# Two changes of order at the end of the second layer: the last third of the token sums goes to POOL's queue behind the last scan, and the weight splits wait for the root of the last pair's normalisation

## The chip, the cores and the metric

The kernel runs as one program on one core of a Trainium2 chip. The metric is the device time of one execution in microseconds (us). Each number below that belongs to an execution is that of the kernel before: three timed runs, and one more that the hardware profiler recorded. The engines are named as the profile names them: PE (TensorE, the matrix products), PEld (its weight loads), DVE (VectorE), ACT (ScalarE), POOL (GpSimd) and SP (SyncE, which here only issues DMAs).

## The reference

Two residual layers work on x of 512 tokens by 2048 channels, in fp32. Layer 0 is gated differential attention. Layer 1, whose end is what this document is about, is a gated RWKV-7 mixer with 32 heads of 64 channels:

```python
def rwkv7_mixer(h, v_first, w_in, mu, ..., gn_w, gn_b, w_out, vres):
    p = h @ w_in
    p = p + (token_shift(p) - p) * mu
    r, k, v, g, dw, da = jnp.split(p, RW_SPLITS, axis=-1)
    ...
    y = wkv7_scan(rh, heads(decay), kh, vh, -kk, kk * ah)
    mean = jnp.mean(y, axis=-1, keepdims=True)
    var = jnp.mean(jnp.square(y - mean), axis=-1, keepdims=True)
    y = (y - mean) * lax.rsqrt(var + GN_EPS)
    y = y * gn_w... + gn_b...
    y = y + jnp.sum(rh * kh * r_k.astype(F32), axis=-1, keepdims=True) * vh
    y = y.reshape(B, T, RW_WIDTH).astype(h.dtype) * jax.nn.silu(g)
    return y @ w_out, v_first
...
out, v_first = rwkv7_mixer(hn, v_first, ...)
x = x + out.astype(x.dtype)
```

So behind the scan each head is centred, divided by its standard deviation, scaled, gated, and the 2048 channels then go through the 2048 x 2048 matrix w_out. Nothing of what is computed is changed here; the change moves work.

## The kernel before

**Products.** An fp32 product is made of three PE passes. Each operand is split into a rounded high part and the rest: for weights, ACT makes the high part `wh` (L110) and DVE the rest `wl` by a subtraction (L111), in `split_w`. `mm3` (L119) then issues wh·hH, wl·hH and wh·hL. The pools of `wh` and of `wl` hold four buffers each; one split of 128x512 weights serves six matmuls of 512 columns. The high and low parts of the mixer's outputs (`yr` and `y`, the rows of the last product) come from ACT (L476) and DVE (L477).

**Layer 1** goes through 16 pairs of heads. For each pair there are projections, a scan over 8 chunks of 64 tokens (`scan_pair`), the outputs `Y` (L1944, L1948), the centring (L1959 to L1961) and the normalisation (`normal`): ACT squares `yc` into `ysq` (L1969), DVE sums it to `var` (L1971), and `rsqrt` (L63 to L70) makes the inverse root in eleven small DVE instructions, the last of which writes `rsg`. `yc` is then scaled by `rsg` (L1977) and transposed on PE (L1989). A chunk of the scan takes a PE product (L1898), an ACT copy `rhs` (L1901), a PE product (L1911), an ACT copy to `VS` (L1913), a PE product (L1920) and a DVE update of `VS` (L1924); POOL copies the state away into `SA` (L1906) and scales it to `Sg` (L1909). The scan of the last pair, 15, runs while the product with w_out has already begun.

**The product with w_out** (`outputs_of`, `Blocks`) is made by a block scheme that saves products: for part of it, it multiplies sums of blocks of weights with sums of blocks of tokens. Both kinds of sums are made from DRAM to DRAM by DMAs (`Sums`). A plain copy is issued on SP's queue (L954), an accumulating add on POOL's (L958). The token sums have four names, s1 to s4 (S1 to S4 where they are loaded), for each of three groups of rows. For a group they take six steps, each of which needs the one before: copy s1 and s3; add to s1 and to s3; copy s1 to s2; add to s2; copy s2 to s4; add to s4. `Forms.load` (L916) brings a sum into SBUF as `fraw`, by a DMA on SP's queue, in the places of a ring that come free one after the other; ACT then makes its high part `fS` (L931) and DVE its low part (L933). In this ring the load of S1's second group waits until S4's third group has been used.

**What sets the order.** Each engine runs its instructions in the order of its own list, which a scheduler makes out of the order in which the program issues work, priorities, and explicit orders (`issue_after` puts an instruction behind another one). An instruction that waits for another engine holds everything behind it in its list. The list of an engine is thus fixed when the kernel is built. In the kernel before, `outputs_of` issues the token sums of the third group one step at a time, at each call of `pace`, spread over the last scan; and the splits of the weights stand in DVE's list where they fall, among the small instructions of the root.

Of the kernel before, what the change touches and what calls it, by code (L numbers as in the profile page):

```python
# [18 lines left out]
ALU = mybir.AluOpType  # L19
# [38 lines left out]
def rsqrt(g, out, v, n, tag):  # L58

    nc = g.nc  # L60
    sh = g.small.tile([P, n], I32, name="rs_i", tag=tag + "i")
    t = g.small.tile([P, n], F32, name="rs_t", tag=tag + "t")
    nc.vector.tensor_single_scalar(sh[:], v.bitcast(I32), 1, ALU.logical_shift_right)  # L63
    nc.vector.tensor_scalar(sh[:], sh[:], -1.0, float(0x5F3759DF), ALU.mult, ALU.add)
    y = sh[:].bitcast(F32)
    for i in range(3):
        nc.vector.tensor_mul(t[:], y, y)
        nc.vector.scalar_tensor_tensor(t[:], t[:], -0.5, v, ALU.mult, ALU.mult)
        o = out if i == 2 else y
        nc.vector.scalar_tensor_tensor(o, t[:], 1.5, y, ALU.add, ALU.mult)  # L70


def load_w(g, raw, block, k0, ks, queue=None):
# [18 lines left out]
@urgent  # L92
def split_w(g, block, kg, cols, k0, raw=None):


    nc = g.nc
    held = raw is not None and block is not None
    if raw is None:
        raw = g.wraw.tile([P, kg, cols], F32, name="wraw", tag="wraw")
        load_w(g, raw, block, k0, slice(0, kg))  # L100
    n = kg // 2
    his, los = [], []
    for k in range(0, kg, n):
        hi = g.wh.tile([P, n, cols], F32R, name="wh", tag="wh")
        lo = g.wl.tile([P, n, cols], F32R, name="wl", tag="wl")
        with ExitStack() as after:
            if held and k0 + k < 4:
                for ins in g.made[k0 + k - 1] if k0 + k else [g.made_prm]:
                    after.enter_context(g.tc.issue_after(ins))
            nc.scalar.copy(hi[:], raw[:, k : k + n])  # L110
            g.split = nc.vector.tensor_sub(lo[:], raw[:, k : k + n], hi[:].bitcast(F32)).ins  # L111
        his.append(hi)
        los.append(lo)
    return Halves(his, n), Halves(los, n)
# [10 lines left out]
class Chain:  # L125
# [17 lines left out]
    def finish(self, g):  # L143
        while self.wait is not None:
            with g.tc.issue_after(g.m.ins):
                self.step(g)
# [337 lines left out]
class Feed:  # L484
# [8 lines left out]
    def load(self, upto):  # L493
        for k in range(len(self.raw), min(upto, self.n)):
            self.raw.append(self.home(k))
            self.g.nc.sync.dma_start(out=self.raw[k], in_=self.src[k * P : (k + 1) * P, :])
# [406 lines left out]
class Forms:  # L903
# [4 lines left out]
        self.at = {nm: [None] * len(homes) for nm in FORMS}  # L908
        self.raw = {}

    def load(self, nm):
        self.raw[nm] = []
        for i in range(len(self.homes)):
            self.ring.append(self.ring.pop(0))
            raw = self.ring[-1]
            self.g.nc.sync.dma_start(out=raw, in_=self.src[FORMS.index(nm), i])  # L916
            self.raw[nm].append(raw)
# [22 lines left out]
class Sums:  # L940
# [1 line left out]


    def __init__(self, g, dr, w, yd):
        self.g, self.w, self.yd = g, w, yd
        N = NS // KG
        self.at = dr.tile([2, 4, N, P, KG, 512], F32, name="wsums")
        self.forms = dr.tile([4, N, P, KG, 256], F32, name="forms")
        self.weights = iter([(i, f) for pair in range(2) for i in range(N) for f in self.weight_sums(pair, i)])
        self.tokens = [(i, f) for i in range(N) for f in self.token_sums(i)]  # L950

    def copy(self, out, src):
        with self.g.tc.issue_after(self.g.loaded):
            self.g.nc.sync.dma_start(out=out, in_=src)  # L954

    def add(self, out, src):
        with self.g.tc.issue_after(self.g.kept):
# [19 lines left out]
    def step(self, m=None):  # L977

        i, f = next(self.weights, (None, None))
        if f is None and self.tokens and self.g.stored >= FIRST[0] + (self.tokens[0][0] + 1) * KG:  # L980
            i, f = self.tokens.pop(0)
        if f:
            f()


class Ring:
# [129 lines left out]
def outputs_of(g, one, two, feed, finish, more):  # L1116


    def pace(n):
        feed(4 + n // 2, g.m)  # L1120
        g.wsums.step()

    def then(nm):
        forms.make(nm)
# [3 lines left out]
    forms, order = one.sums, {"S2": "S4", "S4": "S3"}  # L1128
    N, s = NS // KG, 0
# [15 lines left out]
            one.want("11")  # L1145
            one.take("11", one.y)
    one.take("11", one.X, ALU.subtract)
    forms.load("S1")
    for i in range(N):
        two.first11(i)  # L1150
        if i == 0:
            forms.load("S2")
        if i == 1:
            finish(None)
            more(1)
    two.take("11", two.X, ALU.subtract)
    forms.make("S1", g.m.ins)
    one.rest(then, finish)
# [327 lines left out]
NG = 4  # L1486
# [73 lines left out]


class Pair:
    done, now, scale = False, False, None


def mus(g, i, j):
# [397 lines left out]
def normal(g, p):  # L1964

    nc, w, yc = g.nc, g.work, p.yc
    NG = 2 * NT
# [3 lines left out]
    nc.vector.reduce_sum(var[:], sq[:], AX.X)  # L1971
    nc.vector.tensor_scalar(var[:], var[:], 1.0 / C, GN_EPS, ALU.mult, ALU.add)
    rs = g.small.tile([P, NG], F32, name="rsg", tag="rsg")
    rsqrt(g, rs[:], var[:], NG, "r8")

    def scale():
        nc.vector.tensor_mul(yc[:], yc[:], rs[:, :, None].to_broadcast([P, NG, C]))  # L1977
# [16 lines left out]
def layer1(g, aps):  # L1994
    nc, tc = g.nc, g.tc
    with ExitStack() as cx:
# [38 lines left out]
        for j in range(D // P):  # L2035
# [40 lines left out]
                held = gate(g, j - 1, gps, None)  # L2076
            if j + 1 < D // P:
                r = receptances(j + 1)
        chain(g, j, p, 3, 4, 5, whole=True)
        gts = [held, gate(g, j, proj(3, j), "E")]  # L2080
        feed = Feed(g, g.yd2, KT - 2, lambda k: w.tile([P, T], F32, name="yr", bufs=1, tag=(
# [70 lines left out]
def body(ctx, tc, nc, aps):  # L2152
    g = Ctx()
    g.nc, g.tc = nc, tc
    g.last, g.first, g.ticks, g.kept, g.stored = None, [], 0, None, 0
    g.chains, g.later, g.soon, g.late, g.state, g.solve = [], [], [], [], None, None
    g.hp = ctx.enter_context(tc.tile_pool(name="hp", bufs=16))
    g.wh = ctx.enter_context(tc.tile_pool(name="whp", bufs=4))
# [48 lines left out]
```

## Time and profile before

| what | value |
|---|---|
| median of 3 timed runs | 2070.9 us (2068.37 to 2071.54) |
| the profiled execution, its own time | 2067.63 us |
| its span in the trace | 2065.9 us |
| PE busy | 2044.4 us, 99% of the span |
| DVE busy | 1690.7 us, 82% |
| ACT busy | 1288.6 us, 62% |
| POOL busy | 433.4 us, 21% |
| mean granted clock of PE | 0.999 |

PE is busy nearly throughout, so the time is PE's work plus the few places where PE stands still. In a timeline row the columns are the start in us, the busy time in us, the engine, the line, the operation with output and input, and in brackets how long the engine had been idle before the row and what released it. A row of the windows view gives the stretch, its length, the busy time of PE, PEld, DVE, ACT and POOL with their instruction counts, the clock that was granted to PE (1.00 is full), the mean busy share of the 16 DMA engines, and the GB/s moved. Two instructions on an engine overlap by their start-up, so that a row of matmuls of 0.39 us each advances by less than that.

### The profile page before, as it was taken

To read this page: it belongs to the slowest core of one execution; us is meant where nothing else is said; L and a number is where in the kernel's file an instruction comes from. 1 tells how busy PE (TensorE), PEld (TensorE's weight loads), DVE (VectorE), ACT (ScalarE), POOL (GpSimd) and SP (SyncE) were. 2 spreads that over 40 slices of the span, in tenths; PEclk is the share of its full clock that TensorE was granted. 3 is DMA by queue.
4 is the path that set the end of the run, shared out by engine and by line. 5 is a ranking of instruction groups with operands and counts; after the bars stand their busy time and mean duration, and the time that the engine had idled before them with its cause. 6 is when DMAs were issued, how large, how long until landed. Compare 5 with 4: busy or idle time off the path is not lost.

```text
span 2065.9 us, 35395 instructions
## 1 busy us (share of the span) xinstructions
PE 2044.4 (99%) x11888; PEld 1682.6 (81%) x11888; DVE 1690.7 (82%) x4417; ACT 1288.6 (62%) x3065; POOL 433.4 (21%) x751
## 2 busy tenths in 40 slices
PE   9999999999999999999999999999999999999999
PEld 8888878888888878888778888888888888876787
DVE  5979788897888976576888888888888898887865
ACT  5667676676767754455666666666666666666543
POOL 0020211202111000101232332233333232342000
PEclk9999999999999999999999999999999999999999
DMA  6387877869778665832234443434445332347663
GB/s 201 115 172 184 163 173 175 177 173 168 176 166 212 182 204 180 201 104 95 96 104 131 131 120 97 127 111 130 110 126 136 99 96 86 108 134 214 204 229 133
DMA packets 113943, 306.95 MB, mean 149 GB/s; under 512 B 13920, under 2 KB 35056, under 8 KB 113472
## 3 DMA queue, kind: packets, MB, share of 16 engines
q1 hardware_dynamic: 71056, 204.15, 30.5%
q0 software_dynamic: 28272, 84.52, 23.3%
q10 hardware_dynamic: 14432, 16.01, 2.2%
q8 instruction: 94, 1.54, 0.3%
q14 instruction: 89, 0.73, 0.1%
HBM read 288.63 MB, written 47.45 MB: 163 GB/s over the span
## 4 chain that ended last, share of the span: by engine, by line
PE 43%; DVE 3%; DMA 2%; ACT 1%; issue 1%; SPq 0%; DVEq 0%; ACTq 0%
PE pp L119 31%; PE pt L119 4%; PE sm L1898 1%; PE gp L1669 1%; PE sm L1920 1%; PE sm L1911 1%; DMA forms<-yd 1%; PE Y L1944 1%; DVE wl L111 1%; PE pt L1729 1%; PE px L1796 0%; PE Y L1948 0%; PE px L1811 0%; DMA yr<-yd 0%; PE pt L1989 0%
## 5 line engine op out<-in xcount | busy, mean ns | idle before, releaser
L119 PE MATMUL pp<-hH,wh 128*128 128x512 f32 x1024 | 416.9, 407 | 0.0
L119 PE MATMUL pp<-hL,wh 128*128 128x512 f32 x1024 | 412.1, 402 | 0.0
L119 PE MATMUL pp<-hH,wl 128*128 128x512 f32 x1024 | 411.9, 402 | 0.0
L110 ACT CAST wh<-wraw 128x512 fp32r<-128x512 f32 (+1 forms) x412 | 254.1, 618 | 211.0 <-PE pp L119 139.7
L111 DVE TENSOR_TENSOR wl<-wraw,wh 128x512 fp32r<-128x512 f32 (+1 forms) x412 | 289.9, 705 | 78.2 <-ACT wh L110 73.6
L119 PE MATMUL pp<-wh,hH 128*128 128x512 f32 x784 | 311.7, 398 | 0.7 <-DVE G L383 0.4
L119 PE MATMUL pp<-wl,hH 128*128 128x512 f32 x784 | 308.5, 393 | 0.0
L119 PE MATMUL pp<-wh,hL 128*128 128x512 f32 x784 | 307.8, 393 | 0.0
L119 PEld LDWEIGHTS pp<-hH,wh 128*128 128x128 f32 x1024 | 192.9, 188 | 38.0 <-issue 1.8
L119 PEld LDWEIGHTS pp<-hH,wl 128*128 128x128 f32 x1024 | 193.2, 189 | 33.2
L119 PEld LDWEIGHTS pp<-hL,wh 128*128 128x128 f32 x1024 | 193.2, 189 | 31.3
L119 PE MATMUL pp<-wh,S 128*128 128x512 f32 x672 | 214.4, 394 | 0.0
L616 ACT CAST wh<-T 128x512 fp32r<-128x512 f32 x224 | 137.2, 620 | 91.5 <-PE pp L119 70.9
L1906 POOL COPY SA<-VS 64x64 f32<-64x64 f32 x224 | 76.1, 340 | 494.6 <-DVE VS L1924 446.2
L119 PEld LDWEIGHTS pp<-wh,hH 128*128 128x128 f32 x784 | 147.7, 188 | 31.0 <-DVE acc L1056 0.7
L119 PEld LDWEIGHTS pp<-wh,hL 128*128 128x128 f32 x784 | 148.0, 189 | 30.0
L119 PEld LDWEIGHTS pp<-wl,hH 128*128 128x128 f32 x784 | 147.8, 188 | 28.7 <-DVE wl L111 0.3
L617 DVE TENSOR_TENSOR wl<-T,wh 128x512 fp32r<-128x512 f32 x224 | 150.6, 685 | 23.3 <-ACT wh L616 22.6
L589 POOL DMA_DIRECT2D T<-in_da_w_in_dram x84 | 72.2, 860 | 385.6 <-DMA wraw<-in_da_w_in_dram 193.9
L1762 DVE SCALAR_TENSOR_TENSOR tmpl<-LT,n,Tm 128x60 f32<-128x60 f32 (+24 forms) x496 | 135.9, 274 | 13.3
L119 PEld LDWEIGHTS pp<-wh,S 128*128 128x128 f32 x672 | 124.8, 188 | 24.5
L119 PE MATMUL pp<-wl,S 128*128 128x512 f32 x336 | 132.1, 393 | 0.0
(374 smaller groups left out, 4100.7 us busy)
## 6 DMA issues: line engine op xcount, KB each, us to landing
wraw<-in_rw_w_in_dram SPq DMA_DIRECT2D x128, 512.0 KB, 3.7
T<-in_da_w_in_dram POOLq DMA_DIRECT2D x84, 512.0 KB, 6.7
wraw<-in_da_w_in_dram SPq DMA_DIRECT2D x64, 512.0 KB, 3.9
T<-in_da_w_in_dram SPq DMA_DIRECT2D x28, 512.0 KB, 4.4
wraw<-in_da_w_out_dram SPq DMA_DIRECT2D x26, 512.0 KB, 4.6
wsums<-in_rw_w_out_dram POOLq DMA_DIRECT2D x24, 512.0 KB, 5.9
wraw<-in_da_w_in_dram POOLq DMA_DIRECT2D x21, 512.0 KB, 6.7
wraw<-in_rw_w_out_dram SPq DMA_DIRECT2D x17, 512.0 KB, 4.0
```

Of the source, the lines that this page charges most:

```text
L110: nc.scalar.copy(hi[:], raw[:, k : k + n])
L111: g.split = nc.vector.tensor_sub(lo[:], raw[:, k : k + n], hi[:].bitcast(F32)).ins
L119: m = nc.tensor.matmul(out, a, b, start=s, stop=e, skip_group_check=skip)
L589: self.g.nc.gpsimd.dma_start(out=raw, in_=src, accum_op=ALU.add)
L616: g.nc.scalar.copy(hi[:], raw[:, k])
L617: g.nc.vector.tensor_sub(lo[:], raw[:, k], hi[:].bitcast(F32))
L1669: m = nc.tensor.matmul(gp[h][:, i * P : (i + 1) * P], BK[r_, c0 + i, :, :], p.AR[r_, c0 + i, :, :], start=True, stop=True)
L1729: nc.tensor.transpose(ps[:, i * P : (i + 1) * P], p.BK[:, c0 + i].rearrange("p s t -> p (s t)"), g.ident[:])
L1762: st = nc.vector.scalar_tensor_tensor(tt, LT[:, i : i + 1, i + 1 :].to_broadcast([P, s, n]), n2[:, i : i + 1], Tm[:, 0:s, i : i + 1].to_br ...
L1898: nc.tensor.matmul(sm[:, 0:P], both(p.G[:, c, 0]), both(VS[:, c]), start=True, stop=True)
L1906: g.kept = nc.gpsimd.tensor_copy(p.SA[r_, c - 1, :], VS[r_, c, h, :]).ins
L1911: nc.tensor.matmul(sm[:, P : P + C], both(g.TT[j % 2][:, c]), rhs[:], start=True, stop=True)
```

## The change

There are three edits. First, `rsqrt` returns its last instruction; for the last pair it is kept as `g.root`, and from then on `split_w` puts every weight split's subtraction (`wl`) behind it. Second, `Forms.load` can load part of a name: the third group of S1 and the whole of S2 are now loaded behind the loop over `two.first11`, not ahead of it and within it. Third, `pace` no longer steps the token sums; a new function `finish` issues what is left of them, all eight DMAs of the third group, on POOL's queue, and behind `g.kept`, which by then is the last `SA` copy of the last scan.

```diff
@@ rsqrt
-        nc.vector.scalar_tensor_tensor(o, t[:], 1.5, y, ALU.add, ALU.mult)
+        root = nc.vector.scalar_tensor_tensor(o, t[:], 1.5, y, ALU.add, ALU.mult)
+    return root.ins
@@ split_w
             nc.scalar.copy(hi[:], raw[:, k : k + n])
+            if g.root:
+                after.enter_context(g.tc.issue_after(g.root))
             g.split = nc.vector.tensor_sub(lo[:], raw[:, k : k + n], hi[:].bitcast(F32)).ins
@@ class Forms
-    def load(self, nm):
-        self.raw[nm] = []
-        for i in range(len(self.homes)):
+    def load(self, nm, some=None):
+        if nm not in self.raw:
+            self.raw[nm] = []
+        for i in some or range(len(self.homes)):
             self.ring.append(self.ring.pop(0))
             raw = self.ring[-1]
             self.g.nc.sync.dma_start(out=raw, in_=self.src[FORMS.index(nm), i])
@@ class Sums
     def copy(self, out, src):
-        with self.g.tc.issue_after(self.g.loaded):
-            self.g.nc.sync.dma_start(out=out, in_=src)
+        queue, after = (self.g.nc.gpsimd, self.g.kept) if self.late else (self.g.nc.sync, self.g.loaded)
+        with self.g.tc.issue_after(after):
+            queue.dma_start(out=out, in_=src)
...
+    def finish(self):
+        self.late = True
+        while self.tokens:
+            self.step()
@@ outputs_of
     def pace(n):
         feed(4 + n // 2, g.m)
-        g.wsums.step()
...
-    forms.load("S1")
+    forms.load("S1", range(N - 1))
     for i in range(N):
         two.first11(i)
-        if i == 0:
-            forms.load("S2")
         if i == 1:
             finish(None)
+            g.wsums.finish()
             more(1)
+    forms.load("S1", range(N - 1, N))
+    forms.load("S2")
@@ normal
-    rsqrt(g, rs[:], var[:], NG, "r8")
+    root = rsqrt(g, rs[:], var[:], NG, "r8")
+    if p.last:
+        g.root = root
@@ layer1
+        p.last = True
         chain(g, j, p, 3, 4, 5, whole=True)
```

Lines move by the added text: `wl` is L114 in the kernel after, `fraw` L920, the two halves of `fS` L935 and L937, the copies and adds of the sums L959 and L963, `var` L1981, the scaling L1989.

The first place is POOL's list at the end of the last scan. Before, around the last token sum in the list, it is

```order
L1909 TENSOR_SCALAR Sg<-SA,gam 128x64
L1906 COPY SA<-VS 64x64 x2
L958 DMA forms<-yd_79 256x1x256
L1909 TENSOR_SCALAR Sg<-SA,gam 128x64
L1906 COPY SA<-VS 64x64 x2
```

with only such copies and scalings behind it, and after, to the end of the work,

```order
L1916 COPY SA<-VS 64x64 x2
L959 DMA forms<-yd_79 256x1x256 x2
L963 DMA forms<-yd_79 256x1x256 x2
L959 DMA forms<-forms 16x4096
L963 DMA forms<-yd_79 256x1x256
L959 DMA forms<-forms 16x4096
L963 DMA forms<-yd_79 256x1x256
```

Where single adds stood between the scan's copies, a chain of eight DMAs now stands behind the last of them, in the order copy s1 and s3, add to s1 and to s3, copy to s2, add to s2, copy to s4, add to s4; there is nothing behind it.

The second place is DVE's list from the last centring on. `fS_22348` is the low half of S1's third group, `TT_10298` a buffer of raw weights. Before, it is

```order
L933 SCALAR_TENSOR_TENSOR fS_22348<-fraw,fS_22347 128x512
L477 TENSOR_TENSOR hL<-yr,hH 128x512
L111 TENSOR_TENSOR wl<-TT_10298,wh 128x512
L477 TENSOR_TENSOR hL<-y,hH 128x512
L1959 TENSOR_REDUCE s_22190<-Y 128x4 x2
L1960 TENSOR_SCALAR s_22190<-s_22190 128x4 x2
L1961 TENSOR_TENSOR yc<-Y,s_22190 128x4x64 x2
L111 TENSOR_TENSOR wl<-wraw,wh 128x512
L1971 TENSOR_REDUCE var<-ysq 128x8
L111 TENSOR_TENSOR wl<-wraw,wh 128x512
```

and after

```order
L67 TENSOR_TENSOR rs_t<-rs_i 128x8
L68 SCALAR_TENSOR_TENSOR rs_t<-rs_t,var 128x8
L937 SCALAR_TENSOR_TENSOR fS_22348<-fraw,fS_22347 128x512
L70 SCALAR_TENSOR_TENSOR rs_i<-rs_t,rs_i 128x8
L67 TENSOR_TENSOR rs_t<-rs_i 128x8
L68 SCALAR_TENSOR_TENSOR rs_t<-rs_t,var 128x8
L70 SCALAR_TENSOR_TENSOR rs_i<-rs_t,rs_i 128x8
L67 TENSOR_TENSOR rs_t<-rs_i 128x8
L68 SCALAR_TENSOR_TENSOR rs_t<-rs_t,var 128x8
L70 SCALAR_TENSOR_TENSOR rsg<-rs_t,rs_i 128x8
L114 TENSOR_TENSOR wl<-TT_10298,wh 128x512
L1989 TENSOR_TENSOR yc<-yc,rsg 128x512
```

The splits `wl` have gone behind `rsg`, and the low half of S1's third group has gone from ahead of the centring into the root, between two of its small instructions.

The third place is SP's list in the same stretch. Before, `fraw` of S2's third group follows on a copy of the sums while the scan runs,

```order
L995 DMA T_21730<-in_rw_w_out_dram 128x1024
L954 DMA forms<-forms 16x4096
L916 DMA fraw<-forms 128x512
L995 DMA wraw<-in_rw_w_out_dram 128x1024 x3
```

and after, `fraw` of S1's third group and, in the row of three, that of S2's come between the last loads of plain weights and the first of summed ones:

```order
L1005 DMA T_21730<-in_rw_w_out_dram 128x1024
L1005 DMA wraw<-in_rw_w_out_dram 128x1024 x2
L1005 DMA TT_10299<-in_rw_w_out_dram 128x1024
L1061 DMA acc<-xd 128x512
L920 DMA fraw<-forms 128x512
L1061 DMA acc<-xd 128x512
L920 DMA fraw<-forms 128x512 x3
L1005 DMA TT_10298<-wsums 128x1024
L1005 DMA wraw<-wsums 128x1024
```

The copies of the sums have left this queue, and the loads of S1's third group and of S2 stand later in it.

More of the change, by code (lines that the diff above doesn't have):

```diff
@@ L944, in __init__ @@
     def __init__(self, g, dr, w, yd):
-        self.g, self.w, self.yd = g, w, yd
+        self.g, self.w, self.yd, self.late = g, w, yd, False
         N = NS // KG
@@ L1562 @@
 class Pair:
-    done, now, scale = False, False, None
+    done, now, scale, last = False, False, None, False
 def mus(g, i, j):
@@ L2154, in body @@
     g.nc, g.tc = nc, tc
-    g.last, g.first, g.ticks, g.kept, g.stored = None, [], 0, None, 0
+    g.last, g.first, g.ticks, g.kept, g.stored, g.root = None, [], 0, None, 0, None
     g.chains, g.later, g.soon, g.late, g.state, g.solve = [], [], [], [], None, None
```

## The prediction, made before the changed kernel was run

> **What bounds the kernel now.** I read the page first, then the waits of PE, then the stretch of the last scan by windows, and in the gaps that showed there the timelines of PE, ACT, DVE, POOL and SP.
>
> ```profile
> PE 2044.4 (99%) x11888; PEld 1682.6 (81%) x11888; DVE 1690.7 (82%) x4417; ACT 1288.6 (62%) x3065; POOL 433.4 (21%) x751
> ```
>
> ```profile
> PE sm L1920 <- ACT VS L1913: 3.5, 3, 3.0
> ...
> PE pt L1989 <- DVE yc L1977: 0.7, 1, 0.7
> PE pt L119 <- ACT fS L931: 0.7, 1, 0.7
> ```
>
> PE sets the time, so an edit is worth what it takes from PE's stalls or adds to them. The longest wait for another engine is a single one of 3.0 us. The windows put it into the last scan.
>
> ```profile
> 1900.00:1905.00 5.00, 2.11 (x11) 1.42 (x9) 1.21 (x3) 1.95 (x6) 1.79 (x3) 1.00 0.70 196
> 1905.00:1909.00 4.00, 3.93 (x13) 3.22 (x14) 2.19 (x5) 1.67 (x5) 2.19 (x4) 0.58 0.89 218
> 1909.00:1920.00 11.00, 10.71 (x55) 8.11 (x54) 9.21 (x17) 8.09 (x20) 3.88 (x6) 1.00 0.43 127
> ```
>
> PE works 2.11 of the 5 us from 1900 on, and in the 4 us behind the gap its granted clock is 0.58 (the third number from the end). What held it is seen on the way from POOL to PE, one row from each of POOL, SP, ACT and PE's timelines in the order of the events, SP's in two rows:
>
> ```profile
> 1891.35 1.03 POOL L958 DMA_DIRECT2D forms<-yd  x1
> ```
> ```profile
> 1899.85 0.49 SPq L954 DMA_DIRECT2D forms<-forms  x1
> 1900.39 0.57 SPq L916 DMA_DIRECT2D fraw<-forms  x1
> ```
> ```profile
> 1893.78 0.63 ACT L931 ACTIVATE fS<-fraw 128x512 fp32r<-128x512 f32 x1 [1.11 <-DVE VS L1924]
> ...
> 1903.42 0.63 ACT L931 ACTIVATE fS<-fraw 128x512 fp32r<-128x512 f32 x1 [2.87 <-DMA fraw<-forms]
> ...
> 1904.58 0.44 ACT L1913 COPY VS<-sm 64x64 f32<-64x64 f32 x2
> ```
> ```profile
> 1896.46 0.44 PE L1911 MATMUL sm<-rhs,TT 128*128 128x64 f32 x2 [0.81 <-ACT rhs L1901]
> ...
> 1905.07 0.49 PE L1920 MATMUL sm<-VS,BKT 128*128 128x128 f32 x2 [2.95 <-ACT VS L1913]
> ```
>
> The add to s2 was issued on POOL at 1891.35; the copy to s4 and, behind it on SP, the load of S2's third group could go at 1899.85 and 1900.39, when it had landed; ACT stood at that group's high part until 1903.42, with the scan's copy to VS behind it; PE stood for the scan. The 0.81 us is a smaller case of the same kind.
>
> **What the change removes.** In the list of ACT that it makes, S2's third group no longer stands in the scan: the 2.95 us go (term A), and with them the slow clock that followed, 4.0 us x (1 - 0.58) = 1.7. The activation at 1893.78 (S4's second group) stays where it was, but its load no longer stands on SP behind a copy that waits for an add; I count its 0.81 us as gone (A2). The third is the wait of the transposes for the scaling.
>
> ```profile
> 1934.62 0.16 DVE L67 TENSOR_TENSOR rs_t<-rs_i 128x8 f32<-128x8 f32 x1
> 1934.69 0.68 DVE L111 TENSOR_TENSOR wl<-wraw,wh 128x512 fp32r<-128x512 f32 x1
> 1935.30 0.16 DVE L68 SCALAR_TENSOR_TENSOR rs_t<-rs_t,var 128x8 f32<-128x8 f32 x1
> 1935.49 0.17 DVE L70 SCALAR_TENSOR_TENSOR rsg<-rs_t,rs_i 128x8 f32<-128x8 f32 x1
> 1935.69 0.69 DVE L1977 TENSOR_TENSOR yc<-yc,rsg 128x512 f32<-128x512 f32 x1
> ```
> ```profile
> 1936.44 0.66 PE L1989 MATMUL pt<-ident,yc 128*128 128x128 f32 x4 [0.66 <-DVE yc L1977]
> 1936.85 0.47 PE L119 MATMUL pt<-wh,hH 128*128 128x512 f32 x1
> ```
>
> Two small steps in sequence are 0.20 us apart, and a split between two of them costs some 0.6 more; with the splits held behind the root, PE's wait of 0.66 us for the scaled `yc` goes (B); the four transposes themselves take 0.4. Gains: 2.95 + 1.68 + 0.81 + 0.66 = 6.1 us.
>
> **What the change adds.** DVE's new list has the low half of S1's third group inside the root, and every split behind the root. DVE runs in order. So the splits wait not only for the root but for a load that now waits for POOL: the copy to s1, the add to s1, and the load. None of the three can start before the last SA copy has run.
>
> ```profile
> 1920.44 0.69 POOL L1906 COPY SA<-VS 64x64 f32<-64x64 f32 x1 [0.16 <-DVE VS L1924]
> ```
> ```profile
> forms<-yd POOLq DMA_DIRECT2D x12, 256.0 KB, 5.2
> fraw<-forms SPq DMA_DIRECT2D x12, 256.0 KB, 3.6
> forms<-yd SPq DMA_DIRECT2D x6, 256.0 KB, 3.6
> forms<-forms SPq DMA_DIRECT2D x6, 256.0 KB, 2.9
> ```
> ```profile
> 1903.38 1.11 POOL L958 DMA_DIRECT2D forms<-yd  x1 [3.13 <-DMA forms<-forms]
> ```
>
> These are the end of the SA copies (1921.13), medians from issue to landing over the whole run, and the add that followed the copy issued at 1899.85: with 2.9 us to landing, the copy was there at 1902.75 and POOL's row starts 0.6 later. All adds ran on POOL, all copies on SP; no row shows a copy on POOL's queue. I take 4.4 us for it, midway between SP's 3.6 and POOL's 5.2, and keep 3.1 to 6.9 for the range from single landings:
>
> ```profile
> forms<-yd SPq DMA_DIRECT2D x2, 256.0 KB, 3.1
> ```
> ```profile
> forms<-yd POOLq DMA_DIRECT2D x1, 256.0 KB, 4.6
> ```
> ```profile
> forms<-yd POOLq DMA_DIRECT2D x1, 256.0 KB, 8.5
> ```
> ```profile
> forms<-yd POOLq DMA_DIRECT2D x1, 256.0 KB, 6.9
> ```
> ```profile
> DMA to landing us min/median/max: 2.5/3.6/8.6
> ```
>
> (the copy at 1761; the adds at 1764, 1891 and 1903; and the loads of `fraw`). The last add fell where 0.70 to 0.89 of the DMA engines' time was taken; from 1920 on it is
>
> ```profile
> 1920.00:1930.00 10.00, 9.95 (x98) 7.86 (x97) 9.59 (x23) 6.03 (x13) 0.92 (x2) 1.00 0.75 247
> 1930.00:1940.00 10.00, 9.34 (x44) 7.47 (x43) 8.91 (x22) 4.80 (x9) 0.00 (x0) 1.00 0.68 228
> ```
>
> so I stay with the medians. The load arrives at 1921.1 + 4.4 + 0.6 + 5.2 + 3.6 = 1934.9. Then come ACT's high half (0.63), DVE's low half, seven small steps (7 x 0.20 = 1.4) and the first split:
>
> ```profile
> 1922.20 0.68 DVE L111 TENSOR_TENSOR wl<-TT,wh 128x512 fp32r<-128x512 f32 x1
> 1922.81 0.68 DVE L933 SCALAR_TENSOR_TENSOR fS<-fraw,fS 128x512 fp32r<-128x512 f32 x1
> ```
>
> that is 0.63 + 0.68 + 1.4 + 0.68 = 3.4, and PE has its first held split at 1938.3. When does it want it? At
>
> ```profile
> 1927.45 0.39 PE L119 MATMUL pp<-wh,hH 128*128 128x512 f32 x1
> 1927.68 0.39 PE L119 MATMUL pp<-wl,hH 128*128 128x512 f32 x1
> ```
>
> the products of that buffer begin; PE's new list runs four of their wh·hH matmuls ahead, 0.23 us each, so it stands from 1928.4. **Term C** is 1938.3 - 1928.4 = 9.9 us. (The times are those of before; the gains in the scan shift both ends alike.)
>
> **Term E** is the next wait of that kind. ACT's new list has S2's third group between the two high parts of the buffer `T`. Its load needs copy s2 and add s2 too: add s1 is there at 1931.3, then 0.6 + 4.0 (a copy of sums, between SP's 2.9 and POOL's 5.2) + 0.6 + 5.2 + 3.6 = 1945.3, and with 0.63 each for the two activations the second `wh<-T` is ready at 1946.6. PE wants it when five splits of six matmuls (1.37 us each), less the four run ahead (0.9), and the transposes (0.4) are done: 1938.3 + 6.3 = 1944.6. That is 2.0 us more. The last link, S4's third group, with the load of S1's second group behind it, comes by the same steps about when PE gets there; I count nothing for it, and keep up to 5 us for the range. The four copies and four adds are the same bytes as before, and POOL has nothing else to do.
>
> **Term F**: a stall of 10 us should cost as much clock as the one of 2.95 us did: 1.7 us; between 0 and, if both stalls cost it, 3.4.
>
> Sum: -6.1 + 9.9 + 2.0 + 1.7 = +7.5 us. On the profiled execution (2067.63; 1.7 us of it lie outside the span) that is 2075.1; its time is 3.3 us under the median of the timed runs, 2070.9, so the median I expect is 2070.9 + 7.5 = **2078.4 us**, 0.36% slower.
>
> A rule of the Trainium skill speaks against putting the plain copies on this queue: "DMA: Bandwidth & Descriptors", in the section "SWDGE vs HWDGE vs iDMA", sends plain transfers to SP or ACT and only accumulating, casting or irregular ones to GpSimd; the medians above, 3.6 against 5.2, agree, though they compare copies with adds. Another section, "Anatomy of one DMA — SWDGE (gpsimd) path", has a fit of 2.0 us plus the bytes at 436 GB/s, by which an estimate for 256 KB is 2.6 us; by it the sum would come out near that of the first rival. The shortest add here, 4.6, is longer, so I don't use it.
>
> **The rivals.** *The chain is short* (not slower). With the shortest rows throughout, copy 3.1, add 4.6, load 2.5, the load is there at 1921.1 + 3.1 + 0.6 + 4.6 + 2.5 = 1931.9 and the split at 1935.3: a stall of 6.9, next to nothing left for E, clock 0 to 1.7. The sum is +0.8 to +2.5, about 2072.5 us. It decides once the three DMAs take under 10.5 us together instead of 13.8. For it speaks that the scan's DMA load has ended (share 0.43 from 1909 to 1920); against it, that the shares of 0.75 and 0.68 afterwards aren't low.
>
> *The chain is slow.* Copy 6.9, add 8.5, load 4.5 give a stall of 16.7 and E of about 8, +20 us; halfway there, with the last link's 5 us open, +13: 2084 us. For it: the adds of the last scan took 8.5 and 6.9. Against: they fell into the fullest windows.
>
> *The root alone holds* (faster or the same). If S1's third group were early, the splits still would wait for the root.
>
> ```profile
> 1927.86 0.69 DVE L1971 TENSOR_REDUCE var<-ysq 128x8 f32<-128x512 f32 x1
> ```
>
> From its end, 1928.5, twelve small steps and a split make 1931.6, a stall of 3.2 us: -6.1 + 3.2 = -2.9, or 2068 us. It needs the three DMAs within 7 us, less than any rows give. *The change doesn't do what it says* would be that ACT's stall only moves to another instruction of the scan; ACT's new list has no token sum of the third group before `yc`, so I give that no chance of its own.
>
> **How the numbers follow.** A measurement of this kernel can tell about 0.2%, 4.1 us, from no change. The forecast (the low half of S1's third group holds the splits, with ordinary DMAs) has 0.52, the short chain 0.24, the slow chain 0.14, the root alone 0.10. Slower by over 0.2%, above 2075.0: all of the slow chain and most of the forecast, 0.50, so 0.64. Faster by over 0.2%, below 2066.8: the root alone if some stall that I don't see goes as well, 0.08. The same: 0.28. The likeliest case's own range is 2074 to 2083; the range for 8 in 10 goes from 2069, with most of the short chain inside, to 2087 at the middle of the slow one.
>
> **What would show it.** In the changed kernel's profile, no ACT row inside the last scan waits for `fraw`, and the scan's L1930 has no wait near 3 us. PE has one stall of 7 to 12 us ahead of a `wl` product of L122, released by DVE's `wl` L114; DVE at that time stands before the low half L937, released by ACT's L935 or the DMA `fraw`; POOL's last eight DMAs start right behind the last SA copy. Behind the stall the granted clock falls below 1 for some 4 us. The wait for `yc` at the transposes is gone. It would be wrong if DVE reached the splits with `fraw` already there, if PE's stall were under 5 us, or if the three DMAs took under 10 us.

## The result, and the profile after

The changed kernel is slower: 2082.3 us median (2080.4 to 2086.0) against 2069.8 (2066.8 to 2071.9) for the kernel before, six runs of each. That is 12.5 us more, a ratio of 1.0063 with a 95% interval of 1.0050 to 1.0076. The forecast was 7.5 us slower, a median of 2078.4 us, with a range of 2069 to 2087 us.

The waits of PE in the changed kernel (engine, tile and line that waited, what released it; us in total, times, the longest) have changed places:

```profile
PE pp L122 <- DVE wl L114: 8.7, 1, 8.7
PE sm L1908 <- DVE VS L1934: 3.2, 7, 0.9
PE pt L122 <- ACT wh L111: 3.2, 1, 3.2
PE pt L122 <- ACT fS L935: 2.1, 1, 2.1
```

The wait of 3.0 us in the last scan is gone, and so is the one of the transposes. In their place there are three in the product with w_out. The first, by DVE's timeline:

```profile
1925.40 0.17 DVE L68 SCALAR_TENSOR_TENSOR rs_t<-rs_t,var 128x8 f32<-128x8 f32 x1
1930.80 0.69 DVE L937 SCALAR_TENSOR_TENSOR fS<-fraw,fS 128x512 fp32r<-128x512 f32 x1 [5.23 <-ACT fS L935]
1931.41 0.16 DVE L70 SCALAR_TENSOR_TENSOR rs_i<-rs_t,rs_i 128x8 f32<-128x8 f32 x1
...
1932.61 0.17 DVE L70 SCALAR_TENSOR_TENSOR rsg<-rs_t,rs_i 128x8 f32<-128x8 f32 x1
1932.69 0.68 DVE L114 TENSOR_TENSOR wl<-TT,wh 128x512 fp32r<-128x512 f32 x1
```

DVE stands for 5.23 us in the middle of the root, at the low half of S1's third group, and all splits stand behind the root. POOL's and ACT's timelines give the chain that leads there and goes on to the second stall:

```profile
1916.61 0.69 POOL L1916 COPY SA<-VS 64x64 f32<-64x64 f32 x1 [0.16 <-DVE VS L1934]
1917.30 1.43 POOL L959 DMA_DIRECT2D forms<-yd  x2
1922.25 1.12 POOL L963 DMA_DIRECT2D forms<-yd  x1 [3.53 <-DMA forms<-yd]
1927.70 1.06 POOL L963 DMA_DIRECT2D forms<-yd  x1 [4.33 <-issue]
1928.28 1.01 POOL L959 DMA_DIRECT2D forms<-forms  x1
1935.93 1.06 POOL L963 DMA_DIRECT2D forms<-yd  x1 [6.64 <-DMA forms<-forms]
```
```profile
1930.14 0.63 ACT L935 ACTIVATE fS<-fraw 128x512 fp32r<-128x512 f32 x1 [5.63 <-DMA fraw<-forms]
...
1943.04 0.63 ACT L935 ACTIVATE fS<-fraw 128x512 fp32r<-128x512 f32 x1 [6.83 <-DMA fraw<-forms]
1943.57 0.60 ACT L111 CAST wh<-T 128x512 fp32r<-128x512 f32 x1
```

Copy s1 from 1917.30, add s1 from 1922.25, then S1's third group on ACT at 1930.14; copy s2 from 1928.28, add s2 from 1935.93, then S2's third group on ACT at 1943.04, and behind it the high part of `T` that PE wants. PE's timeline shows both stalls and what follows each:

```profile
1933.43 0.80 PE L122 MATMUL pp<-wl,hH 128*128 128x512 f32 x1 [8.73 <-DVE wl L114]
1934.02 0.63 PE L122 MATMUL pp<-wh,hL 128*128 128x512 f32 x1
1934.45 0.63 PE L122 MATMUL pp<-wl,hH 128*128 128x512 f32 x1
...
1936.53 0.40 PE L122 MATMUL pp<-wh,hL 128*128 128x512 f32 x1
1936.77 0.39 PE L122 MATMUL pp<-wl,hH 128*128 128x512 f32 x1
...
1944.23 0.79 PE L122 MATMUL pt<-wh,hH 128*128 128x512 f32 x1 [3.17 <-ACT wh L111]
...
1965.10 0.50 PE L122 MATMUL pt<-wh,fS 128*128 128x512 f32 x1 [2.14 <-ACT fS L935]
```

Right behind a stall the matmuls come 0.43 us apart; some 3 us later behind the first, and some 6 behind the second, they come 0.23 apart. In the windows view this is the granted clock (a mean over the whole stretch, PE's idle time included):

```profile
1930.00:1940.00 10.00, 6.57 (x23) 5.32 (x24) 6.66 (x16) 1.88 (x3) 1.06 (x1) 0.68 0.67 144
1940.00:1950.00 10.00, 6.83 (x20) 4.94 (x19) 4.75 (x8) 3.32 (x6) 1.55 (x2) 0.66 0.73 251
```

To set the two profiled executions against each other, a common point is needed that lies ahead of the change. Such a point is the first product for `Y` of the pair before the last, of before and of after:

```profile
1876.08 1.09 PE L1944 MATMUL Y<-VS,G 128*64 128x64 f32 x29
```
```profile
1877.71 1.20 PE L1954 MATMUL Y<-VS,G 128*64 128x64 f32 x32
```

The changed execution is 1.6 us late there already, without any change ahead. From there to the start of the last SA copy it takes 38.9 us in place of 44.4, so 5.5 less. From that copy to the end (spans 2079.4 and 2065.9) it takes 162.8 us in place of 145.5, so 17.3 more: 8.7 and 3.2 for the first two stalls, 1.5 for the third (2.14, where 0.65 stood before), less 0.7 for the transposes, and a rest of 4.6. PE's rows put this rest down to the slow clock. Behind the first stall seven matmuls take 3.1 us (1933.43 to 1936.53), where at 0.23 each they would take 1.6. Behind the second, eleven matmuls and the four transposes take 6.0 us (1944.23 to 1950.19), where at 0.23 each and 0.4 for the transposes they would take 2.9. The net of 11.8 agrees with the timed 12.5.

### The profile page after: what moved, and what is told of

Its sections match the earlier page's. It is cut to its first block, busy times and chain, and to the rows that moved or that the text cites. A ratio compares the mean times of both kernels' runs of the same rounds, so it can differ in the third digit from the quotient of the medians.

```text
span 2079.4 us, 35400 instructions
## 1 busy us (share of the span) xinstructions
PE 2048.6 (99%) x11888; PEld 1683.9 (81%) x11888; DVE 1690.2 (81%) x4417; ACT 1288.9 (62%) x3065; POOL 438.3 (21%) x755
## 4 chain that ended last, share of the span: by engine, by line
PE 44%; DVE 2%; DMA 2%; issue 1%; ACT 1%; POOL 0%; DVEq 0%; ACTq 0%; POOLq 0%
PE pp L122 31%; PE pt L122 5%; PE sm L1908 1%; PE sm L1930 1%; PE gp L1679 1%; PE sm L1921 1%; PE Y L1954 1%; DVE wl L114 1%; DMA forms<-yd 1%; PE pt L1739 0%; PE px L1821 0%; PE px L1806 0%; PE Y L1958 0%; DMA fraw<-forms 0%; DMA forms<-forms 0%
## 5 line engine op out<-in xcount | busy, mean ns | idle before, releaser
L114 DVE TENSOR_TENSOR wl<-wraw,wh 128x512 fp32r<-128x512 f32 (+1 forms) x412 | 289.6, 705 | 75.1 <-ACT wh L111 70.5
```

## The experiments

Two theories stood against each other at the start. One is that of the prediction: the token sums come too late, in a serial chain. The other is that the hold itself costs, since every later split stands behind the root. A table of all timed runs first; each ratio is to the kernel before on the same chip.

| kernel | median us | against before, us | ratio, 95% interval |
|---|---|---|---|
| the change | 2082.3 | +12.5 | 1.0063 (1.0050 to 1.0076) |
| e1 hold only | 2070.4 | +0.6 | 1.0008 (0.9999 to 1.0017) |
| e2 change without hold | 2080.9 | +11.1 | 1.0058 (1.0045 to 1.0071) |
| e3 change, copies on SP | 2078.6 | +8.7 | 1.0046 (1.0033 to 1.0058) |
| e4 change, low half behind the root | 2080.7 | +10.9 | 1.0055 (1.0041 to 1.0068) |
| e5 scan gain alone | 2067.9 | -1.9 | 0.9991 (0.9982 to 0.9999) |
| e6 change, add to s3 last | 2078.7 | +9.0 | 1.0042 (1.0029 to 1.0055) |
| e7 e3 once more, one run | 2077.9 | +8.1 | one run, no interval |
| e8 scan gain and hold | 2072.4 | +2.7 | 1.0012 (1.0003 to 1.0021) |
| e9 scan gain, only the add to s4 late | 2064.6 | -4.3 | 0.9982 (0.9973 to 0.9991) |
| e10 e9 and hold from the fifth split | 2065.3 | -3.7 | 0.9986 (0.9977 to 0.9994) |
| e11 e3 and the add to s3 last | 2074.6 | +5.7 | 1.0027 (1.0017 to 1.0037) |
| e12 e10 and S1's low halves behind the root | 2064.0 | -5.9 | 0.9972 (0.9961 to 0.9982) |

### The two halves of the change: e1 and e2

The third edit, the place of the loads in the program, has no run of its own: with that edit alone the lists of all engines are the same as before, row for row but for the numbers of buffers. What it does beside the other two is not tried by itself. So the change has two halves.

e1 is the kernel before with the hold:

```diff
+            if g.root:
+                after.enter_context(g.tc.issue_after(g.root))
             g.split = nc.vector.tensor_sub(lo[:], raw[:, k : k + n], hi[:].bitcast(F32)).ins
```

> The hold alone: the splits wait for the root as in the change, while the token sums, the loads and their queues stay as before. Theory (the late token sums hold PE; the hold by itself costs only what the root takes): S1's third group is ready long before, so PE stands some 3 us ahead of the first held split, the 2.95 us stall in the last scan stays, the 0.66 us wait for yc goes, and the clock takes 0 to 1.7 us; +2.5 to +4.5 us against before. Rival (the hold itself costs, since every later split stands behind the root): most of the +12.5 us is here, +9 or more.

Measured: +0.6 us, not to be told from no change (interval -0.2 to +3.5). The profile shows the stall that was expected, and the one in the scan still there:

```profile
PE sm L1923 <- ACT VS L1916: 3.2, 3, 2.7
PE pp L122 <- DVE wl L114: 2.9, 1, 2.9
```

The rival falls: here the hold costs nothing near 12 us. Its cost is under what was expected; e8 will give it once more.

e2 is the changed kernel without those two lines.

> The changed kernel without the hold: token sums late on POOL, splits free. Theory: DVE still has the low half of S1's third group inside the root with the splits of the next buffer behind it, and ACT has its high half ahead of that buffer's high parts; PE gets four splits further (5.5 us), then stands for the same chain; the first stall falls to 3 to 6 us, the stall at S2's third group stays or grows; +9 to +12 us against before. Rival (the hold itself costs): only the gain in the scan is left, -4 to -6 us.

Measured: +11.1 us. Nearly the whole loss is there without the hold; the stall of 8.7 us is only spread over more places (the two largest are 2.5 us for `wh` and 2.1 us for `yc`, since the root now ends late):

```profile
PE pt L120 <- ACT wh L111: 3.4, 2, 2.5
PE pt L120 <- DVE wl L112: 3.3, 3, 1.7
...
PE pt L1999 <- DVE yc L1987: 2.1, 1, 2.1
...
PE pt L120 <- DVE acc L1064: 1.9, 1, 1.9
```

So the late sums are the cause, and the hold mostly decides where PE stands for them: 11.1 us without it and 12.5 with it are not told apart by their intervals.

### Which part of the late chain: e4, e3, e6, e11

e4 queues the low halves of S1 behind the root, so that the third group's no longer stands inside it, and leaves the sums as late as they were:

```diff
-    forms.make("S1", g.m.ins)
+    forms.make("S1", g.root)
```

> The changed kernel with the low half of S1's third group queued behind the root on DVE, not inside it; token sums as late as in the change. Theory A (the whole serial chain of sums sets the time): the first stall falls from 8.7 to 3 to 5 us, and PE then comes earlier to the split whose high part stands on ACT behind S2's third group, where it stands 6 to 8 us in place of 3.2; nearly the same total, +10 to +13 us against before. Theory B (the low half's place inside the root is the cost by itself): the 5 us are gained, +6 to +8.

Measured: +10.9 us; theory A holds. The first stall falls from 8.7 to 2.9 us, and ACT takes over: it stands at the same `fraw`, now with the high parts of `T` behind it.

```profile
PE pt L122 <- ACT wh L111: 6.1, 2, 3.1
PE pp L122 <- DVE wl L114: 2.9, 1, 2.9
PE pt L122 <- ACT fS L935: 2.8, 1, 2.8
```

e3 puts the four plain copies back on SP's queue. SP's list has no SA copy in it, so the first two copies go at 1864, about where they go before the change.

```diff
-        queue, after = (self.g.nc.gpsimd, self.g.kept) if self.late else (self.g.nc.sync, self.g.loaded)
+        queue, after = (self.g.nc.sync, self.g.kept) if self.late else (self.g.nc.sync, self.g.loaded)
```

> The changed kernel with the four plain copies of the last group on SP's queue again (the adds stay on POOL behind the last scan). The first copies then need not wait for the scan's end, and a copy takes SP's 3 to 4 us in place of 4.5 to 7. Theory (length of the serial chain of DMAs): the chain to S1's third group loses the copy's 4.9 us, so the first stall is 3 to 5 us, the one at S2's third group goes, the gain in the scan stays; -2 to +2 us against before. Rival (the hold itself costs, whichever queue the copies use): +8 or more.

Measured: +8.7 us. This expectation missed its range by 6.7 us. e7, one more run of the same kernel, gave 2077.9 us:

> Placeholder of the same kernel as the run with copies on SP: a second look at its profile; first stall 5 to 6.5 us, the add to s3 again starts right behind the landing of the add to s1.

The time is that which the rival names, but it doesn't speak for it, since the hold by itself is cheap in e1, and in e2 the loss stays without it. The profile of e3 shows two reasons. The first stall is 5.8 us, not 3 to 5: the low half is still inside the root, and the add and the load before it still start behind the last SA copy. And POOL's timeline with SP's beside it shows a link that the prediction did not have:

```profile
1917.77 1.14 POOL L963 DMA_DIRECT2D forms<-yd  x1
1923.93 1.07 POOL L963 DMA_DIRECT2D forms<-yd  x1 [5.02 <-issue]
1932.20 1.03 POOL L963 DMA_DIRECT2D forms<-yd  x1 [7.20 <-issue]
```
```profile
1923.62 0.50 SPq L959 DMA_DIRECT2D forms<-forms  x1
```

The copy to s2 started at 1923.62 and took 3.0 us, so the add to s2 (the third row) could have started at 1926.6. It started at 1932.20. Ahead of it in POOL's list is the add to s3, which started at 1923.93 and took 7.9 us, to 1931.8. Nothing in the program makes the add to s2 wait for s3: they are different sums. Two kernels test it, both with the add to s3 as the last DMA of the chain:

```diff
+        if i == NS // KG - 1:
+            return [lambda: (self.copy(s1, b), self.copy(s3, a)), lambda: self.add(s1, d),
+                    lambda: self.copy(s2, s1), lambda: self.add(s2, a), lambda: self.copy(s4, s2),
+                    lambda: self.add(s4, c), lambda: self.add(s3, b)]
```

(each late add is ordered behind the one before, so that the scheduler keeps this order). e6 does it to the changed kernel, e11 to e3.

> The changed kernel with one DMA of the eight moved: the add to s3, which stood behind the add to s1 and ran beside the copy to s2, comes last. Theory (an add on POOL's queue and a copy beside it slow each other, and the next add waits): the first stall stays 8 to 9 us; copy to s2 lands in 4 to 5 us in place of 7.2, add to s2 starts 3 us earlier, so the stall at S2's third group falls from 3.2 to under 1 us and the one at S1's second group from 2.1 to under 1; +7 to +9 us against before. Rival (the length is set by the steps of the chain alone, the add to s3 is free): as the change, +11 to +13.

> The changed kernel with its four copies on SP and, beside that, the add to s3 as the last DMA on POOL. In the run with the copies on SP alone, the add to s2 started at 1932.2, when the add to s3 had landed (8.3 us), though its own copy had landed 5 us before. Theory (an add on POOL's queue waits for the landing of the add ahead of it, so the add to s3 was a link of the chain): the add to s2 starts when the copy to s2 has landed, about 3.5 us behind the landing of the add to s1; the stall at S2's third group (1.7 us) goes, the first one stays at 4.5 to 6; +4 to +6.5 us against before. Rival (the add to s2 waits for something else): as with the copies on SP, +7.5 to +9.5.

e6 measured +9.0 us, 3.5 less than the change. The first stall is 8.3 us, near the change's 8.7; the copy to s2 lands in 4.4 us in place of 7.2 and the add to s2 starts at 1931.46 in place of 1935.93; the stall for S2's third group is gone. Not all of it is gained: PE waits 2.7 us for `acc` later on. The landing of the copy to s2, in the change and in e6:

```profile
forms<-forms POOLq DMA_DIRECT2D x1, 256.0 KB, 7.2
```
```profile
forms<-forms POOLq DMA_DIRECT2D x1, 256.0 KB, 4.4
```

and POOL's rows of e6:

```profile
1921.42 1.12 POOL L963 DMA_DIRECT2D forms<-yd  x1 [3.58 <-DMA forms<-yd]
1926.64 0.53 POOL L959 DMA_DIRECT2D forms<-forms  x1 [4.10 <-DMA forms<-yd]
1931.46 1.05 POOL L963 DMA_DIRECT2D forms<-yd  x1 [4.29 <-DMA forms<-forms]
...
1940.60 1.07 POOL L963 DMA_DIRECT2D forms<-yd  x1 [3.85 <-DMA forms<-forms]
1949.27 1.05 POOL L963 DMA_DIRECT2D forms<-yd  x1 [7.60 <-issue]
```

The last row is the add to s3 once more: nothing is left for it to wait for, and it starts 8.7 us behind the add to s4, which took 8.4. e11 measured +5.7, 3.0 less than e3; there the add to s2 starts at 1926.59, 3.4 us behind the landing of the add to s1, with no stall at S2's third group. So the add to s3 held up the chain in both kernels, in two ways: in the change it ran beside the copy to s2, which then took longer, and the add to s2 waited for that copy; in e3 the add to s2 waited for the add to s3 itself. (By the times alone each of the two steps is likely rather than shown, since the intervals of e6 and the change, and of e11 and e3, overlap at their ends; the rows show it.)

### Whether the aim can be had without the late chain: e5, e8, e9, e10, e12

e5 measures the gain in the scan by itself: in the kernel before, ACT's high parts of S2 and S4 go behind the last scan's last copy to VS.

```diff
+        g.scanned = vc.ins
...
-            nc.scalar.activation(hi, v, AF.Copy, scale=sign)
+            with self.g.tc.issue_after(self.g.scanned) if nm in ('S2', 'S4') else ExitStack():
+                nc.scalar.activation(hi, v, AF.Copy, scale=sign)
```

> The kernel before with one order added: ACT's high parts of S2 and S4 go behind the last scan's last copy to VS. No hold, token sums as before. It measures the gain A of the prediction by itself. Theory: the 2.95 us stall in the scan and the slow clock behind it go and nothing takes their place: -3 to -6 us against before. Rival (the scan's own chain of engines takes the freed time, or S2 and S4 come late at the product): -1 to +1.

Measured: -1.9 us (interval -3.7 to -0.2). That lies between the two values expected: ACT's wait goes, and another one shows that it had hidden. Here are rows of POOL, DVE and PE of e5:

```profile
1903.80 1.11 POOL L959 DMA_DIRECT2D forms<-yd  x1 [3.74 <-DMA forms<-forms]
1904.99 0.44 POOL L1910 TENSOR_SCALAR Sg<-SA,gam 128x64 f32<-128x64 f32 x1
```
```profile
1905.46 0.60 DVE L1926 SCALAR_TENSOR_TENSOR VS<-sm,gam,Sg 64x64 f32<-64x64 f32 x2 [3.25 <-POOL Sg L1910]
```
```profile
1906.21 0.46 PE L1899 MATMUL sm<-VS,G 128*128 128x128 f32 x2 [2.56 <-DVE VS L1926]
```

POOL stands 3.74 us for the copy to s4, with the add to s4 next in its list; the scan's `Sg` is behind the add, DVE's update of VS waits for `Sg`, and PE for VS. The same row is in the prediction for the kernel before (the add at 1903.38, 3.13 us idle); there ACT's wait covered it. From the first product for `Y` of the pair before the last to the last SA copy, the kernel before takes 44.4 us, e5 42.1 and the change 38.9. So moving the sums out of POOL's list did earn something that ACT's list alone does not give.

e8 is e5 with the hold of e1.

> The kernel before with the hold and with ACT's high parts of S2 and S4 behind the last scan, so both gains of the change without its late token sums. Theory: the gain of the scan alone plus the +0.6 us that the hold cost by itself: -2.5 to -5 us against before. Rival (hold and scan gain overlap): slower than the scan gain alone by 3 us or more.

Measured: +2.7 us, 4.6 above e5. The expectation missed, and what the rival names (3 us or more above e5) came. The stall ahead of the first held split is 2.9 us as in e1, and there the clock falls as well (0.85 from 1930 to 1940). Taken with e1 the hold costs 0.6 to 4.6 us, where 2.5 to 4.5 was expected of it in e1. Why it costs more here isn't shown. The clock has a part in it: five runs of e8 took 2068.1 to 2070.7 us with a mean granted clock of 0.999 or 1.000, the other six 2072.4 to 2074.4 with 0.997 or 0.998.

e9 adds to e5 that the last of the token sums, the add to s4 alone, goes behind the last SA copy; the seven DMAs ahead of it stay where they were.

```diff
+    def finish(self):
+        while self.tokens:
+            i, f = self.tokens.pop(0)
+            f()
...
-        if f is None and self.tokens and self.g.stored >= ...
+        if f is None and len(self.tokens) > 1 and self.g.stored >= ...
...
             finish(None)
+            g.wsums.finish()
             more(1)
```

> The kernel before with two orders added: ACT's high parts of S2 and S4 behind the last scan (as in the scan gain alone), and of the token sums only the last one, the add to s4, behind the last SA copy on POOL. No hold. Theory (the scan stood behind two engines: ACT at S2's third group and, hidden by it, POOL at the add to s4, which holds the scan's Sg): the 2.6 us wait of the scan's L1899 for DVE's VS goes too; the last SA copy comes 3.5 to 5.5 us earlier than before, S4 still comes in time; -3.5 to -5.5 us against before. Rival (the rest of the scan's chain sets its pace, or the late add to s4 holds S4): -2 or less gain, as without it.

Measured: -4.3 us (interval -5.6 to -1.9). PE's wait of 2.6 us in the scan is gone, the stretch up to the last SA copy takes 39.6 us, nothing waits for S4, and the largest wait left in this part of PE's timeline is

```profile
1934.85 0.66 PE L1997 MATMUL pt<-ident,yc 128*128 128x128 f32 x4 [1.46 <-DVE yc L1985]
```

This is the wait that the hold is for. e10 lets the first four splits go free and holds the others behind the root:

```diff
+            if g.root:
+                g.free -= 1
+                if g.free < 0:
+                    after.enter_context(g.tc.issue_after(g.root))
...
+    if p.last:
+        g.root, g.free = root, 4
```

> The kernel of the run before in this call with the hold as well, but only for splits from the fifth on: the first four, which PE wants while the root runs, go free. Theory (the hold costs because PE wants the first held split 3 us before the root can end; four splits are 5.5 us of products): no stall ahead of a held split over 0.5 us, the wait of the transposes for yc (0.7 to 1.3 us) goes; 0.5 to 1.5 us under the run without hold. Rival (any hold moves the wait to the next split): a stall of 1 to 3 us ahead of the first held split, 1 us or more above the run without hold.

Measured: -3.7 us, not to be told from e9, where 0.5 to 1.5 us less was expected. The wait for `yc` is gone, but PE stands 1.75 us ahead of the first held split, as the rival has it, and DVE shows why: the mechanism of the change once more, with another group of S1.

```profile
1929.55 0.69 DVE L939 SCALAR_TENSOR_TENSOR fS<-fraw,fS 128x512 fp32r<-128x512 f32 x1 [1.65 <-ACT fS L937]
1930.16 0.16 DVE L67 TENSOR_TENSOR rs_t<-rs_i 128x8 f32<-128x8 f32 x1
```

e12 queues S1's low halves behind the root too, by the edit of e4.

> The kernel of the hold from the fifth split on, with the low halves of S1 queued behind the root too. In that run PE stood 1.75 us ahead of the first held split, because DVE stood 1.65 us inside the root at the low half of S1's first group, whose load was late: the mechanism of the change, smaller. Theory: with that half out of the root, no stall over 0.5 us ahead of a held split and none at the transposes; 1 to 2 us under the run with the hold from the fifth split on, -4.5 to -6.5 us against before. Rival (the wait moves to ACT or to S1's product): the same time within 0.7 us.

Measured: -5.9 us, a ratio of 0.9972 (0.9961 to 0.9982): faster than both kernels. No wait for a held split and none for `yc` is left. Against e10 it is 2.2 us better by the differences to before; the intervals of the two overlap, so that step by itself is likely and not shown.

## Why the prediction was right, and where it was off

**The sign and the mechanism** were right, and 2082.3 us lies inside the forecast's own range of 2074 to 2083, at its upper end. The chain copy s1, add s1, load, high half, low half inside the root, rest of the root, first held split is what PE's longest stall waits for, and its rows stand in the expected order. e4 shows, however, that "the low half inside the root" is only where the chain strikes first: with it out of the way, ACT's list brings nearly the same total. The prediction had this second place as a term of its own and did not see that the two can stand in for each other.

**The terms**, forecast and measured in the profiled executions:

| term | forecast us | measured us |
|---|---|---|
| gain in the scan (A with its clock, and A2) | -5.4 | -5.5 |
| transposes' wait for yc (B) | -0.7 | -0.7 |
| first stall (C) | +9.9 | +8.7 |
| stall at S2's third group (E) | +2.0 | +3.2 |
| S4's and S1's last links | 0 (up to 5) | +1.5 |
| clock behind the stalls (F) | +1.7 (0 to 3.4) | about +4.6, as a rest |
| sum | +7.5 | +11.8 |

C came out 1.2 us under its forecast, mostly because the load took 2.7 us and not 3.6. The copy to s1 on POOL's queue took 4.5 us (5.3 is the median of the pair issued together), and the add started 4.95 us behind it, close to the 4.4 + 0.6 of the sum. That the assumed 4.4 held is in part luck: the prediction says that no row shows a copy on POOL's queue, but the page of before has one plain load on both queues, the 512 KB of `T<-in_da_w_in_dram`, with 6.7 us on POOL's and 4.4 on SP's, and a price nearer to the first would have been as well founded.

**A step that failed** is in E: "add s1 is there at 1931.3, then 0.6 + 4.0 (a copy of sums ...) + 0.6 + 5.2". It leaves the add to s3 out. The prediction counted eight DMAs and then followed a chain of six steps, as if the two adds of a step ran side by side. By e6 and e11 the add to s3 belongs to the chain: beside it the copy to s2 took 7.2 us and not 4.0, and without it the stall at S2's third group goes. E was only 1.2 us off because other terms went the other way: the add to s2 took 4.5 us and not 5.2, its load 2.6 and not 3.6, and PE, on a slow clock, wanted the split 7.6 us behind the first held one and not 6.3. A sign of it was there to be read: before the change, too, one add starts just when the one ahead has landed.

**The clock** was the largest miss, 2.9 us. F priced a stall at 1.7 us whatever its length, from one case, and took one stall; there were two that cost it, and slow clock lasted 3.0 us behind the first and 5.8 us behind the second. The prediction named the case of two (up to 3.4) and set it aside; even that falls short of 4.6.

**The gain in the scan** came out as forecast in this pair of executions, but that agreement is partly luck, and e1 and e5 show that its parts were not understood. The clock term is not in every execution: e1, whose scan has the same order as before, has a stall of 2.7 us at the same place with a granted clock of 1.00 behind it, and its stretch up to the last SA copy takes 42.5 us where the profiled execution of before took 44.4. Against e1 the change gains 3.6 us there and not 5.5. And the prediction put the gain down to ACT alone, where POOL's add to s4 stood behind it with nearly as long a wait. ACT's order alone gave 1.9 us (e5), both together 4.3 (e9); POOL's alone was not run.

**The rivals.** The short chain (not slower) didn't happen: its three DMAs would have had to take under 10.5 us and took 12.8 (4.95, 5.1 and 2.7). The slow chain didn't happen for S1, and one link of it did for S2 (the copy, 7.2). The root alone appears in e1, where the stall is 2.9 us against the 3.2 forecast.

## What to carry to other kernels

An order that holds work behind a result holds it behind everything that the scheduler has put ahead of that result: before adding such a hold, read the list up to that result for anything that waits for a transfer. Work moved off a busy stretch into a serial chain needs its last start computed back from its first reader: here the last of the eight DMAs (the add to s4) had the slack to go behind the scan, and moving that one, with ACT's high parts of S2 and S4, gained 4.3 us, where moving all eight, with the hold, lost 12.5. How many more could go was not run. And a stall that is removed should be followed by asking which other engine was waiting beside it, since a second wait of nearly the same length can be hidden behind the first, as here.

## What the runs showed of the hardware that had not been expected

**Accumulating DMAs on POOL's queue go one at a time.** In each pair of adds that follow on each other, the second starts 0.3 to 0.4 us behind the landing of the first, though the profile shows nothing that it waits for ("issue" as the releaser): 1922.25 + 5.1 and 1927.70 in the change, 1923.93 + 7.9 and 1932.20 in e3, 1940.60 + 8.4 and 1949.27 in e6, 1936.10 + 5.2 and 1941.64 in e11; and in the kernel before, with the landing of the first beside them,

```profile
1764.49 1.15 POOL L958 DMA_DIRECT2D forms<-yd  x1
1769.42 1.08 POOL L958 DMA_DIRECT2D forms<-yd  x1 [3.78 <-issue]
```
```profile
forms<-yd POOLq DMA_DIRECT2D x1, 256.0 KB, 4.6
```

Plain copies on that queue don't do this: two were issued within 1.43 us at 1917.30, and one 0.6 us behind an add at 1928.28. Why adds wait isn't shown by any run. With no add beside it, a copy of the sums (256 KB) took 3.7 to 5.0 us on POOL's queue (the change, e2, e4, e6; the pair issued together in the change has a median of 5.3) and 2.8 to 4.1 on SP's. With an add beside it, a copy on POOL's queue took 7.2 us in the change, 7.5 in e4 and 9.9 in e2, and the add about as long; one on SP's took 2.8 to 5.6. Whether the copy also makes the add longer is not shown: adds with no copy beside them took 4.5 to 9.3 us.

**Slow clock behind a stall.** Behind some stalls PE's matmuls came at about half their rate: 1933.4 to 1936.4 in the change, 1932.9 to 1936.4 in e1 (from 1.0 us behind the restart on), 1929.9 to 1932.7 in e8, and 1944.2 to 1949.9 behind the second stall of the change. Read in stretches of 0.2 us, the granted clock is 1.00 or 0.50, and each time it stays at 0.50 for 3.4 us or a whole multiple of that: 3.4 in the kernel before (1905.7 to 1909.1), e1 (1933.1 to 1936.5) and e8, 6.8 at each of the change's two stalls (1929.6 to 1936.5 and 1943.3 to 1950.1), 10.2 in e6. In the change it has thus halved already while PE stands, and only the part behind the restart costs time. The length of the stall does not decide it alone: one of 2.70 us in e6, 2.91 in e1 and 2.94 in e8 had half clock behind it, those of 2.56 in e5, 2.66 in e1, 2.80 and 2.92 in e4 had not. So a stall of that length may go either way here; where the clock falls, it costs some 1.5 us, and behind the second stall of the change it cost 3.1. The Trainium skill, "TensorE: Matmul & The Clock Gate", in the section "Part 1: The HAM clock gate (the "warmup" mystery)", has half the clock after an idle window of about 3.4 us, and the full clock after about 3.4 us of work. The half rate and the 3.4 us agree; the stalls that were enough, such as the 2.70 us in e6, are shorter than the page has it.
